# Moving the second half of a value projection, and spreading output-weight splits and turned rows, in a fused hybrid decoder layer

## The chip, the cores and the metric

The kernel runs on one core of a Trainium2 chip. The metric is the device time of one execution in microseconds (us). Five engines work side by side, each through its own queue in order: TensorE (PE; matmuls and transposes, its weight loads are listed as PEld), VectorE (DVE), ScalarE (ACT), GpSimd (POOL) and SyncE (SP), which issues the DMAs. The trace is that of one profiled execution.

## What is computed

The layer takes x (1024 tokens of 1024 values, float32). The reference, cut to what matters here:

```python
h = rmsnorm(x, mix_pre_norm)
proj = h @ w_in
q_a, k_a, v_a, q_h, f_h, i_h, g_h = split(proj)
attn = rmsnorm(dilated_mixture_attention(q_a, k_a, v_a, slopes), attn_out_norm)   # 8 heads of 64
rec = hgrn2_recurrence(q_h, f_h, i_h, g_h, lower_bounds, hgrn_out_norm)           # 4 heads of 128
mixed = concatenate([attn, rec]) @ w_out
x = x + rmsnorm(mixed, mix_post_norm)
h = rmsnorm(x, mlp_pre_norm)
x = x + rmsnorm(square(relu(h @ w_ff1)) @ w_ff2, mlp_post_norm)
```

The three dilated windows of the attention are one causal softmax with a table of biases per head, so that a head's block of 128 queries has scores against all earlier keys. The product is float32: each operand is split in a high part (float32r) and the rest, and three matmuls make one product (`three_pass`, L86: high x high, high x low, low x high).

## The kernel before, in words

The whole layer is one function, `hymba_layer`, and the order of all work is written out by hand: each engine gets its instructions in the order in which the program names them. Four stages follow each other: the recurrent heads, the attention loop (from about 314 to 564 us), the output projection with the norms, and the feed-forward part.

**The attention loop** (L970 to L996) has 64 steps: head `hd` = step // 8, block `b` = step % 8 of 128 queries. In step s the program names, in this order: the exponentials of step s + 1 on ACT (`raise_`); the scores of step s + 2, two matmuls per 512 keys on PE, then bias and maximum on DVE (`look`, `score`, L660); the transposes of step s's probabilities on PE, with the high part taken out of the bank by ACT (L708) and the low part by DVE (L709) (`turn`); after odd blocks, a step later, the product with the values (`weigh`, L713), and another step later its transposes back (`finish`, L728), which DVE sums (`anat`, L737) and POOL scales (L738). Then come the step's *hook*, if it has one, and `fill`.

**Filler.** `fill(ns)` (L170) takes pieces of work from a queue of generators. It adds ns to a debt and calls the first generator until the yielded costs have used the debt up; what a piece costs too much is carried to the next step, and what is left when the queue is empty is forgotten. `drain` (L183) runs the queue empty. Before, a step's budget is 3400 - 360 b up to step 43, 1000 in steps 44 to 47, and 1300 from step 48.

The filler of a pair of heads is the next pair's projection, `attn_proj` (L583): query, value and key, each for two halves of 512 tokens (`proj_t`, L329: eight pieces of three matmuls, cost 650 each). DVE scales each finished half by the row norms (`qf`, `vf`, `kf`). A value half is also transposed on PE (`v_turn`, L605, bank `pvt`), and ACT (L611) and DVE (L612) write its high and low parts to `v`. In both value halves that turn stands some pieces after the scaling (L618, L637). A key half goes through `keys_off` (L570): DVE's scaling, two copies on ACT (L576), two subtractions on POOL (L577), four DMA copies. The second key half of a pair waits in `put_off` until a block 7, 0 or 1 (L993). The last pair (number 3, heads 6 and 7, steps 48 to 63) is projected from step 30 on; its scores begin with `look(48)` in step 46, and values of the second half of the tokens are first needed in step 54.

When the last pair's first key half is done, `early_rows` (L755) puts into the space of the first half of the normed input the finished recurrent rows of 512 tokens (`erows`), a gain row, and room for turned rows (`emt`).

**The output projection's first half** is the filler of the last pair: `early_out` (L837), for four blocks of 128 tokens and two halves of the columns, four pieces each (32 in all, cost 650), multiplies a turned recurrent row with output-weight tiles 0 to 3. It needs the rows multiplied by their gain (`row_rec`, L781, POOL), turned (`row_turn`, L811: four transposes on PE into a bank of tag `t`, one of two that the probabilities' transposes use as well; split by ACT and DVE into `emt`), and the weight tiles split.

**Weights** come through one stream (L95 to L164): `w_load` issues the DMA of a tile into one of two buffers `raw`, `w_split` splits it (ACT L83, DVE L84) into the tile that the stream names for it and issues the next load, and `w_get(i, ahead)` (L123) splits up to tile i + ahead. Where the stream names no tile, the parts go to `wh` and `wl`, two buffers each; the output weights have `WO_TAG` (L154) for that.

**The hooks** (L953) are a table of what each step names after its attention work. Those around the change:

Of the kernel before, what the change touches and what calls it, by code (L numbers as in the profile page):

```python
# [12 lines left out]
ALU = mybir.AluOpType  # L13
# [5 lines left out]
T = 1024  # L19
# [6 lines left out]
AH = 8  # L26
# [9 lines left out]
def hymba_layer(ctx, tc, x, w_in, w_out, w_ff1, w_ff2, g_pre, lb_logits, g_mix, g_post,  # L36
                g_mlp, g_mlp_post, bias_tab, level_masks, ident_in, fold_in, out):
    nc = tc.nc
    V, S, G, TE = nc.vector, nc.scalar, nc.gpsimd, nc.tensor
# [18 lines left out]
    def half(name, dtype=F32):  # L58
        return sp.tile([P, 512], dtype, tag="half", name=name, bufs=2)
# [63 lines left out]
    def w_get(i, ahead=1):  # L123
        while done[1] < min(i + 1 + ahead, len(stream)):
            w_split()
        return parts[i]
# [17 lines left out]
    for h in range(HH):  # L144
        dest, box = pair_dest(f"wig{h}")
# [5 lines left out]
    for i in range(4 * HH, 4 * HH + 3 * (AH // 2)):  # L151
        stream.append((w_in[i], None))
    WO0 = len(stream)
    WO_TAG = (None, ("S", "S"), None, ("S", "BT"), ("S", "S"), ("S", "T"), ("T", "T"), ("T", "T"))  # L154

    def wo_dest(k, tags):
        return lambda: (slab(tags[0], f"woh{k}", F32R), slab(tags[1], f"wol{k}", F32R))
# [9 lines left out]
    queue = []  # L167
    debt = [0.0]

    def fill(ns):  # L170
        debt[0] += ns
        while debt[0] > 0 and queue:
            try:
                cost = next(queue[0])
            except StopIteration:
                queue.pop(0)
                continue
            if cost is None:
                break
            debt[0] -= cost  # L180
        debt[0] = min(debt[0], 0.0)

    def drain():  # L183
        while queue:
            n = len(queue)
            fill(1e9)
            assert len(queue) < n or not queue
# [141 lines left out]
    def proj_t(w, name, hf, out_box):  # L329
        wh, wl = kc(w[0]), kc(w[1])  # L330
        pm = bank("mm", f"pm_{name}{hf}")
        for k in range(NK):
            three_pass(pm, (wh[:, k], wl[:, k]), part(hT, k, hf), k == 0, k == NK - 1)
            out_box[0] = pm
            if k < NK - 1:
                yield 650.0
# [228 lines left out]
    first_done = [False] * (AH // 2)  # L565
    A0 = 4 * HH

    put_off = []

    def keys_off(pr, stacks, pm, hf):  # L570

# [11 lines left out]
    def attn_proj(pr):  # L583
        stacks = [{}, {}]
        box = [None]
        w = w_get(A0 + 3 * pr)
        for i in range(2):
            stacks[i]["q"] = slab("S", f"q{pr}_{i}", F32R)
        for hf in range(2):
            sl = slice(hf * 512, hf * 512 + 512)  # L590
            yield from proj_t(w, f"aq{pr}", hf, box)
            full = half(f"qf{pr}{hf}")
            V.scalar_tensor_tensor(full, box[0], 0.125, rrow[:, sl], op0=ALU.mult, op1=ALU.mult)
            lo = half(f"ql{pr}{hf}", F32R)
            for i, (a, b) in enumerate(halves):
                S.activation(stacks[i]["q"][a:b, sl], full[a:b], AF.Copy)
                G.tensor_tensor(out=lo[a:b], in0=full[a:b], in1=f32(stacks[i]["q"][a:b, sl]), op=ALU.subtract)
            nc.sync.dma_start(out=f32(stacks[0]["q"][64:128, sl]), in_=f32(lo[0:64]))
            nc.sync.dma_start(out=f32(stacks[1]["q"][0:64, sl]), in_=f32(lo[64:128]))
            yield 650.0  # L600
        w = w_get(A0 + 3 * pr + 1)
        vs = slab("V8", f"v{pr}", F32R, (P, NT, 2, 2, 64))
        late = None

        def v_turn(full, hf):  # L605
            pt = bank("mm", f"pvt{pr}{hf}")
            for j in range(4):
                TE.transpose(pt[:, j * P:(j + 1) * P], full[:, j * P:(j + 1) * P], ident)
            ptv = pt.rearrange("p (j h d) -> p j h d", j=4, h=2)
            dst = vs[:, hf * 4:hf * 4 + 4]  # L610
            S.activation(dst[:, :, :, 0, :], ptv, AF.Copy)  # L611
            V.tensor_tensor(out=dst[:, :, :, 1, :], in0=ptv, in1=f32(dst[:, :, :, 0, :]), op=ALU.subtract)  # L612
        for hf in range(2):
            sl = slice(hf * 512, hf * 512 + 512)
            n = 0
            for cost in proj_t(w, f"av{pr}", hf, box):
                n += 1
                if n == 4 and late is not None:  # L618
                    v_turn(*late)
                    cost += 450.0  # L620
                yield cost
            full = half(f"vf{pr}{hf}")
            V.tensor_tensor(out=full, in0=box[0], in1=rrow[:, sl], op=ALU.mult)
            late = (full, hf)
            yield 650.0
        while pr > 0 and not first_done[pr - 1]:
            yield None
        w = w_get(A0 + 3 * pr + 2)
        for i in range(2):
            stacks[i]["kh"] = slab("S", f"kh{pr}_{i}", F32R)  # L630
            stacks[i]["kl"] = slab("S", f"kl{pr}_{i}", F32R)
        for hf in range(2):
            sl = slice(hf * 512, hf * 512 + 512)
            n = 0
            for cost in proj_t(w, f"ak{pr}", hf, box):
                n += 1
                if n == 3 and hf == 0:  # L637
                    v_turn(*late)
                    cost += 450.0
                yield cost  # L640
            if hf == 0 and pr == AH // 2 - 1:
                early_rows()
            if hf == 0 or pr == 0:
                keys_off(pr, stacks, box[0], hf)
            else:
                put_off.append((pr, stacks, box[0], hf))
            pairs[pr] = (stacks, vs)
            yield 650.0
# [6 lines left out]
    def load_bias(hd):  # L655
        if hd < AH and hd not in bts:
            bts[hd] = slab("BT", f"bt{hd}") if hd < AH - 1 else early["table"][:, 0]
            nc.sync.dma_start(out=bts[hd], in_=bias_tab[hd])
# [89 lines left out]
    def load_gain(name, tag, src):  # L748
        gains[name] = slab(tag, name)
        nc.sync.dma_start(out=gains[name], in_=src.partition_broadcast(P))  # L750
# [16 lines left out]
    def early_sums():  # L767
        early["sum"] = [wide.tile([P, 2, D], F32, tag="A", name=f"esum{q}") for q in range(NE // 2)]
# [12 lines left out]
    def row_rec(t):  # L781
        gain = gains["early"] if t < NE else gains["gmix"][:, :AW]
        G.tensor_tensor(out=rec_row(t), in0=rec_row(t), in1=gain, op=ALU.mult)
# [27 lines left out]
    def row_turn(t, which, late=False):  # L811

        if t < NE and which == 0:
            dst = early["mt"][t // 2][:, t % 2]
        else:
            if (t, 1) not in mts and (t, 0) not in mts or t < NE:
                mts[t] = slab("V8", f"mt{t}", F32R, (P, 2, 2, 4, P))
            dst = mts[t][:, which]
        mts[t, which] = dst
        src = rec_row(t) if which == 0 else rows[t][:, AW:]  # L820
        pt = bank("pv" if late else "t", f"pmt{t}_{which}")
        for j in range(4):
            TE.transpose(pt[:, j * P:(j + 1) * P], src[:, j * P:(j + 1) * P], ident)
        split_into(dst[:, 0], dst[:, 1], pt.rearrange("p (j c) -> p j c", j=4))
# [119 lines left out]
    for h in range(HH):  # L944
# [5 lines left out]
        if not last:  # L950
            drain()

    hooks = {  # L953
        45: lambda: [row_rec(0), row_rec(1)],
        46: lambda: [w_get(WO0, 0), row_rec(2), row_rec(3)],
        47: lambda: [row_turn(0, 0), w_get(WO0 + 1, 0), load_bias(AH - 1)],
        48: lambda: [drain(), load_gain("gmix", "R", g_mix), early_sums(), w_get(WO0 + 2, 0), row_turn(1, 0),
                     queue.extend(early_out(t) for t in range(NE))],
        49: lambda: [w_get(WO0 + 3, 0), row_turn(2, 0)],
        50: lambda: row_turn(3, 0),  # L960
        55: lambda: [row_load(t) for t in range(3)],
        59: lambda: [row_norm(0), row_gain(0)],
        60: lambda: [row_norm(1), row_gain(1)],
# [6 lines left out]
    for s in range(n_steps):  # L970
        if s % 16 == 6:
            first_done[s // 16] = True
        hd, b = steps[s]
        ready, to_weigh = to_weigh, []
        raise_(s + 1)
        fresh = (s + 2) % 16 == 0
        if not fresh:
            look(s + 2)
        turn(hd, b, exped.pop(s))
        if b % 2:  # L980
            to_weigh.append((hd, b // 2))
        to_fold, last_fold = [(i, g, weigh(i, g)) for i, g in ready], to_fold
        if fresh and s + 2 < n_steps:
            while pairs[(s + 2) // 16] is None:
                fill(1.0)
            if (s + 2) // 16 + 1 < AH // 2:
                drain()
                queue.append(attn_proj((s + 2) // 16 + 1))
            look(s + 2)
        for i, g, a in last_fold:  # L990
            finish(i, g, *a)
        hooks.get(s, lambda: None)()
        if b in (7, 0, 1):  # L993
            while put_off:
                keys_off(*put_off.pop())
        fill(3400.0 - 360.0 * b if s < n_steps - 20 else 1000.0 if s < n_steps - 16 else 1300.0)  # L996
    for i, g, a in to_fold:
        finish(i, g, *a)
    to_fold = [(i, g, weigh(i, g)) for i, g in to_weigh]
# [804 lines left out]
```

## Time and profile before

| | |
|---|---|
| median of 3 runs | 1278.68 us (1278.18 to 1279.29) |
| profiled execution | 1281.3 us |
| its span, from the first to the last instruction | 1279.2 us |
| mean granted clock of TensorE | 0.994 |
| DMA | 153.98 MB, mean 120 GB/s |
| weight-tile split on ACT, 128 x 1024 (L83, `woh`) | 1.06 us each |
| weight-tile split on DVE, 128 x 1024 (L84, `wol`) | 1.22 us each |

How to read the views. A row of a group or of the timeline has the line of the kernel, the engine, the operation, what it writes and reads by the program's names without their numbers, the size, and (in brackets) how long the engine was idle before it and what ended that. In a timeline row the first two numbers are the start and the length, in us from the start of the span; instructions of one kind that follow each other are one row with a count. A row of the windows view has its two ends and its length, then the busy time of PE (and, where all engines are shown, of PEld, DVE, ACT and POOL) with a count, the granted clock, the share of the DMA engines and GB/s. The page's clock row has one digit for each fortieth of the span, 9 for 90% or more. A DMA row ends with the kilobytes of one issue and the median time to its landing. Matmuls overlap in the records, so that a matmul's length is more than the distance to the next one's start.

### The profile page before, as it was taken

How to read it: one execution, taken by the hardware profiler on the slowest of the kernel's cores; microseconds unless marked ns; L12 is line 12 of the kernel's file. 1: busy time of each engine (PE TensorE's matmuls, PEld its weight loads, DVE VectorE, ACT ScalarE, POOL GpSimd, SP SyncE). 2: the span in 40 equal slices, each digit the busy share in tenths (PEclk: the TensorE clock that was granted, in tenths of full speed). 3: DMA queues.
4: the chain of work that ended last, by engine and by line, in shares of the span. 5: the costliest groups of instructions: out<-in, count | busy, mean ns of one | idle time of the engine just before them, and what ended most of it. 6: DMA issues, size and time to landing. Idle time of an engine off the chain costs nothing. (4 is left out here: it accounts for less than half of the span.)

```text
span 1279.2 us, 17265 instructions
## 1 busy us (share of the span) xinstructions
PE 1243.7 (97%) x6512; PEld 1059.0 (83%) x6512; DVE 884.4 (69%) x1530; ACT 533.2 (42%) x969; POOL 291.2 (23%) x304
## 2 busy tenths in 40 slices
PE   9999999999999998999999999999999999999997
PEld 8898989888888887787888888888878888888886
DVE  5686868675666666666668767666675776698956
ACT  7523232213555555564565322222235533344412
POOL 0000000012122223134351387566541000000002
PEclk9999999999999999898999999999999999999999
DMA  5201111123232223326242544344369453534413
GB/s 207 67 17 50 34 51 33 34 82 84 66 83 67 79 71 94 116 90 204 83 166 91 174 172 170 137 170 152 140 242 354 148 200 130 164 99 132 155 68 140
DMA packets 58578, 153.98 MB, mean 120 GB/s; under 512 B 4992, under 2 KB 12928, under 8 KB 58240
## 3 DMA queue, kind: packets, MB, share of 16 engines
q1 hardware_dynamic: 58496, 152.89, 35.8%
q8 instruction: 51, 0.84, 0.3%
q14 instruction: 31, 0.25, 0.1%
HBM read 106.73 MB, written 39.85 MB: 115 GB/s over the span
## 5 line engine op out<-in xcount | busy, mean ns | idle before, releaser
L87 PE MATMUL f<-bh,ah 128*128 128x512 f32 x392 | 152.5, 389 | 0.0
L88 PE MATMUL f<-bl,ah 128*128 128x512 f32 x392 | 152.5, 389 | 0.0
L89 PE MATMUL f<-bh,al 128*128 128x512 f32 x392 | 152.5, 389 | 0.0
L84 DVE TENSOR_TENSOR al<-ar,ah 128x1024 fp32r<-128x1024 f32 x49 | 60.6, 1236 | 48.1 <-ACT ah L83 17.7
L88 PEld LDWEIGHTS f<-bl,ah 128*128 128x128 f32 x392 | 73.6, 188 | 15.4
L87 PEld LDWEIGHTS f<-bh,ah 128*128 128x128 f32 x392 | 73.6, 188 | 15.2
L89 PEld LDWEIGHTS f<-bh,al 128*128 128x128 f32 x392 | 73.6, 188 | 15.1
L83 ACT ACTIVATE ah<-ar 128x1024 fp32r<-128x1024 f32 x49 | 52.1, 1063 | 49.3 <-DMA ar<-actd 20.5
L1719 POOL TENSOR_SCALAR fp<-fss 128x1 f32<-128x1 f32 x8 | 3.5, 434 | 267.4 <-ACT fd L1716 267.4
L681 DVE CUSTOM_DVE_ANT_0 p<-ps,bt 128x512 f32<-128x512 f32 (+2 forms) x84 | 44.3, 552 | 24.2 <-PE ps L679 24.0
L709 DVE TENSOR_TENSOR ptl<-pt,pth 128x512 fp32r<-128x512 f32 (+2 forms) x96 | 50.2, 551 | 15.6 <-ACT pth L708 15.6
L708 ACT ACTIVATE pth<-pt 128x512 fp32r<-128x512 f32 (+2 forms) x96 | 43.3, 486 | 41.7 <-PE pt L705 40.0
L692 ACT ACTIVATE p<-p,nm 128x128 f32<-128x128 f32 (+3 forms) x64 | 49.5, 773 | 9.5 <-DVE nm L687 6.2
L1232 POOL TENSOR_TENSOR e<-x,e 128x512 f32<-128x512 f32 x14 | 20.6, 1475 | 136.3 <-DVE x L1183 136.3
L738 POOL TENSOR_TENSOR anat<-anat,rd 128x128 f32<-128x128 f32 x32 | 14.6, 455 | 150.1 <-DVE anat L737 146.5
L83 ACT ACTIVATE bh<-br 128x1024 fp32r<-128x1024 f32 x28 | 29.8, 1063 | 43.5 <-PE f L89 38.2
L79 POOL TENSOR_SCALAR ms<-hss 128x8 f32<-128x8 f32 x4 | 0.8, 198 | 206.3 <-DVE hss L549 206.3
L705 PE MATMUL pt<-ident,p 128*128 128x128 f32 x288 | 42.9, 276 | 4.7 <-DVE ptl L709 4.7
L84 DVE TENSOR_TENSOR wl<-raw,wh 128x1024 fp32r<-128x1024 f32 x23 | 31.4, 1365 | 18.3 <-ACT wh L83 18.0
L705 PEld LDWEIGHTS pt<-ident,p 128*128 128x128 f32 x288 | 33.5, 141 | 9.3 <-DVE ptl L709 6.8
L722 PE MATMUL pov<-pth,v 128*128 128x256 f32 (+1 forms) x160 | 40.6, 288 | 0.0
L1586 DVE TENSOR_TENSOR acc<-f,acc 128x512 f32<-128x512 f32 x52 | 33.8, 685 | 8.3 <-PE f L89 8.3
(1615 smaller groups left out, 3892.1 us busy)
## 6 DMA issues: line engine op xcount, KB each, us to landing
ar<-actd SPq DMA_DIRECT2D x49, 512.0 KB, 3.6
raw<-in_w_in_dram SPq DMA_DIRECT2D x28, 512.0 KB, 3.5
w1r<-in_w_ff_dram SPq DMA_DIRECT2D x14, 1024.0 KB, 6.3
br<-in_w_ff_dram SPq DMA_DIRECT2D x14, 1024.0 KB, 7.8
actd<-e SPq DMA_DIRECT2D x17, 768.0 KB, 4.1
actd<-e SPq DMA_DIRECT2D x11, 1024.0 KB, 4.0
xr<-in_x_dram SPq DMA_DIRECT2D x8, 512.0 KB, 9.4
raw<-in_w_out_dram SPq DMA_DIRECT2D x8, 512.0 KB, 3.7
```

What stands on the lines that cost most here:

```text
L83: S.activation(hi, src, AF.Copy)
L84: eng.tensor_tensor(out=lo, in0=src, in1=f32(hi), op=ALU.subtract)
L87: TE.matmul(dst, lhs[0], rhs[0], start=start, stop=False)
L88: TE.matmul(dst, lhs[0], rhs[1], start=False, stop=False)
L89: TE.matmul(dst, lhs[1], rhs[0], start=False, stop=stop)
L681: V.tensor_tensor_reduce(out=pe[:, k0:k0 + n], in0=pS[:, :n], in1=bts[hd][:, o:o + n], scale=1.0, scalar=-3.0e38, op0=ALU.add, op1=ALU.max ...
L692: S.activation(pe[:, :nk], pe[:, :nk], AF.Exp, bias=nm[:, b:b + 1], accum_out=dn[:, b:b + 1])
L705: TE.transpose(pt[:, j * P:(j + 1) * P], pe[:, jj * P:(jj + 1) * P], ident)
L708: S.activation(hi, src, AF.Copy)
L709: V.tensor_tensor(out=lo, in0=src, in1=f32(hi), op=ALU.subtract)
L722: TE.matmul(po[:, c0:256], vst, pt[j // 4][q][:, j % 4, c0:], start=j == 0 and q == 0, stop=j == nj - 1 and q == 1)
L1586: V.tensor_tensor(out=acc_at(p, i), in0=pm, in1=acc_at(p, i), op=ALU.add)
```

## The change

The last pair's value projection of the second half of the tokens is taken out of `attn_proj` into a generator of its own, `v_rest`, which step 45 puts into the queue after draining it; `v_turn` follows its scaling directly. The hooks that were in steps 45 to 50 are spread over steps 43 to 53, with one weight tile or one turned row in most of them. The tiles of `wh` and `wl` go to output-weight tiles 2 and 3 instead of 0 and 2, since the value weights now stay in theirs up to step 48, and the last key weights are fetched without one ahead. The second key half is also taken off in step 46. The budgets change: 2660 - 280 b in steps 30 to 43, 1000 in steps 44 and 45, and 1500 from step 46.

```diff
-    WO_TAG = (None, ("S", "S"), None, ("S", "BT"), ("S", "S"), ("S", "T"), ("T", "T"), ("T", "T"))
+    WO_TAG = (("S", "S"), ("S", "BT"), None, None, ("S", "S"), ("S", "T"), ("T", "T"), ("T", "T"))
...
-    put_off = []
+    put_off, deferred = [], []
...
-        for hf in range(2):
+        split = pr == AH // 2 - 1
+
+        def v_rest(wv):
+            sl = slice(512, T)
+            yield from proj_t(wv, f"av{pr}", 1, box)
+            full = half(f"vf{pr}1")
+            V.tensor_tensor(out=full, in0=box[0], in1=rrow[:, sl], op=ALU.mult)
+            yield 650.0
+            v_turn(full, 1)
+            yield 450.0
+        if split:
+            deferred.append(v_rest(w))
+        for hf in range(1 if split else 2):
...
-        w = w_get(A0 + 3 * pr + 2)
+        w = w_get(A0 + 3 * pr + 2, 0 if split else 1)
...
-        45: lambda: [row_rec(0), row_rec(1)],
-        46: lambda: [w_get(WO0, 0), row_rec(2), row_rec(3)],
-        47: lambda: [row_turn(0, 0), w_get(WO0 + 1, 0), load_bias(AH - 1)],
-        48: lambda: [drain(), load_gain("gmix", "R", g_mix), early_sums(), w_get(WO0 + 2, 0), row_turn(1, 0),
+        43: lambda: [row_rec(0), row_rec(1)],
+        44: lambda: [row_rec(2), row_rec(3)],
+        45: lambda: [drain(), queue.append(deferred.pop())],
+        46: lambda: load_bias(AH - 1),
+        47: lambda: w_get(WO0, 0),
+        48: lambda: row_turn(0, 0),
+        49: lambda: w_get(WO0 + 1, 0),
+        50: lambda: [drain(), load_gain("gmix", "R", g_mix), early_sums(), w_get(WO0 + 2, 0), row_turn(1, 0),
                      queue.extend(early_out(t) for t in range(NE))],
-        49: lambda: [w_get(WO0 + 3, 0), row_turn(2, 0)],
-        50: lambda: row_turn(3, 0),
+        51: lambda: w_get(WO0 + 3, 0),
+        52: lambda: row_turn(2, 0),
+        53: lambda: row_turn(3, 0),
...
-        if b in (7, 0, 1):
+        if b in (7, 0, 1) or s == 46:
             while put_off:
                 keys_off(*put_off.pop())
-        fill(3400.0 - 360.0 * b if s < n_steps - 20 else 1000.0 if s < n_steps - 16 else 1300.0)
+        if s < n_steps - 20:
+            fill(3400.0 - 360.0 * b if s < n_steps - 34 else 2660.0 - 280.0 * b)
+        else:
+            fill(1000.0 if s < n_steps - 18 else 1500.0)
```

## The prediction

> **What bounds the kernel now.** I read the page first: busy shares, then the clock row.
>
> ```profile
> span 1279.2 us, 17265 instructions
> ...
> PE 1243.7 (97%) x6512; PEld 1059.0 (83%) x6512; DVE 884.4 (69%) x1530; ACT 533.2 (42%) x969; POOL 291.2 (23%) x304
> ...
> PEclk9999999999999999898999999999999999999999
> ```
>
> TensorE sets the time: it is idle for only 1279.2 - 1243.7 = 35.5 us. A change that neither adds nor removes matmuls, as this one, can win only idle time of PE and time at a lowered clock. One of the two dips of the clock row (slice 17, from 512 us) lies in the attention loop. So I cut the windows view at the steps of that loop (steps 46, 47 and 49; each begins with its score matmuls), and took the idle times of PE from its timeline.
>
> ```profile
> 499.26:502.65 3.39, 2.41 (x22) 2.42 (x22) 2.70 (x10) 2.58 (x6) 1.67 (x3) 1.00 0.00 0
> 502.65:505.56 2.91, 1.93 (x19) 1.72 (x18) 2.25 (x10) 1.85 (x5) 2.91 (x3) 1.00 0.00 0
> ...
> 509.79:518.14 8.35, 4.13 (x17) 2.50 (x16) 5.51 (x13) 6.32 (x15) 3.78 (x3) 0.85 1.02 303
> ```
>
> ```profile
> 500.24 0.98 PE L705 MATMUL pt<-ident,p 128*128 128x128 f32 x7 [0.98 <-DVE ptl L709]
> 505.18 0.63 PE L823 MATMUL pmt<-ident,erows 128*128 128x128 f32 x4 [0.98 <-POOL erows L783]
> 511.72 0.44 PE L705 MATMUL pt<-ident,p 128*128 128x128 f32 x2 [1.32 <-DVE ptl L709]
> 514.52 0.63 PE L823 MATMUL pmt<-ident,erows 128*128 128x128 f32 x4 [2.14 <-issue]
> 514.91 0.48 PE L87 MATMUL pwe<-wh,emt 128*128 128x512 f32 x1
> ...
> 517.12 0.79 PE L88 MATMUL pwe<-wol,emt 128*128 128x512 f32 x1 [0.75 <-DVE wol L84]
> ```
>
> Steps 46 and 47 have no filler matmuls, and PE waits 0.98 us in each. In step 49 it waits 1.32, 2.14 and 0.75 us. Together 6.17 us. What it waits for in step 49 stands in the timelines of DVE and ACT:
>
> ```profile
> 508.56 0.68 DVE L574 TENSOR_TENSOR kf<-pm_ak,rrow 128x512 f32<-128x512 f32 x1
> ...
> 512.60 1.22 DVE L84 TENSOR_TENSOR wl<-raw,wh 128x1024 fp32r<-128x1024 f32 x1 [0.86 <-ACT wh L83]
> 513.74 0.68 DVE L84 TENSOR_TENSOR emt<-pmt,emt 128x512 fp32r<-128x512 f32 x1
> ...
> 515.86 1.21 DVE L84 TENSOR_TENSOR wol<-raw,woh 128x1024 fp32r<-128x1024 f32 x1
> ```
>
> ```profile
> 509.27 1.28 ACT L576 ACTIVATE kh<-kf 64x512 fp32r<-64x512 f32 x2 [1.89 <-DVE kf L574]
> ```
>
> The 1.32 us come from the second half of the keys: ACT stands 1.89 us for `kf` and then works 1.28 us before it gets to the next weights. The 2.14 us ("issue" in the row) end when DVE, done with a weight tile at 513.8, has emptied the bank of the row turned before (`emt`, to 514.42). The 0.75 us end with `wol` at 517.07: an output-weight tile whose split stands in the step that first uses it. Then comes the clock. In PE's windows, cut where the clock changed:
>
> ```profile
> 501.96:505.37 3.41, 2.43 (x22) 1.00 0.00 0
> 505.37:508.79 3.42, 3.42 (x29) 1.00 0.01 2
> 508.79:512.20 3.41, 2.09 (x12) 1.00 0.73 227
> 512.20:515.61 3.41, 1.27 (x9) 1.00 1.07 273
> 515.61:519.03 3.42, 2.67 (x8) 0.50 0.99 332
> 519.03:522.44 3.41, 3.41 (x16) 0.50 0.79 251
> ...
> 594.12:597.53 3.41, 1.44 (x10) 1.00 0.98 310
> ```
>
> After a window with 1.27 us of PE work the granted clock is 0.50 for 6.83 us. Of these PE is idle 0.75, so 6.08 us of work run at half speed and cost 3.04 us. The other dip follows 1.44 us of work; 2.09 and 2.43 us of work caused none. **The prize is 6.17 + 3.04 = 9.2 us**, between 499 and 523 us.
>
> **The change part by part.** PE's work is the same. A filler piece (three matmuls of 512 columns) is the distance of these starts, 0.69 us:
>
> ```profile
> 479.20 0.39 PE L87 MATMUL pm_av<-hTh,wh 128*128 128x512 f32 x1
> ...
> 479.89 0.39 PE L87 MATMUL pm_ak<-hTh,wh 128*128 128x512 f32 x1
> ```
>
> *Steps 30 to 43, fewer pieces.* Counting the new budgets (costs 650 a piece, debts carried) gives 2, 1, 4, 4, 3, 3, 2, 2, 2, 1, 3, 4, 3, 3, 1 pieces in steps 30 to 44 (40 with step 45's two) instead of 2, 2, 5, 5, 4, 3, 3, 3, 1, 1, 6, 4, 4, 3, 2 (48). Where DVE has most to do (steps 37 to 39) at most one is lost. The thin place is the change of weights from query to value, where before PE waits once already:
>
> ```profile
> 461.20 0.50 PE L678 MATMUL ps<-kh,q 128*128 128x512 f32 x1 [1.17 <-DVE mx L681]
> ```
>
> The second query half now ends a step later and has about 0.4 us less PE work behind it before a score needs DVE: +0.4 us, bounds 0 and +1.2 (the wait once more).
>
> *Steps 45 to 47.* Two key pieces and two value pieces, then two, then three: 2.76, 1.38 and 2.07 us of cover where there was none, and the row gains on POOL end four steps before the first row is turned. The two waits of 0.98 us go. The keys' second half moves to step 46, ahead of the crowd, so the 1.32 us go too. What moves onto other queues (the last number is the time to landing):
>
> ```profile
> raw<-in_w_out_dram SPq DMA_DIRECT2D x3, 512.0 KB, 5.1
> erows<-mixd SPq DMA_DIRECT2D x2, 512.0 KB, 8.1
> ...
> kl<-kl SPq DMA_DIRECT2D x4, 128.0 KB, 4.7
> ```
>
> The row gains stand on POOL two steps earlier, behind rows that take 8.1 us to land: POOL waits there, and of what is queued behind it PE needs nothing before step 50. The keys' copies have four steps for their 4.7 us. The load of the fourth output tile leaves when the second is split (step 49) and lands 5.1 us later, about when its split comes up; a microsecond late costs PE as much. It now stands ahead of the gain row's load on SP's queue, which nobody needs before step 59.
>
> *Step 48.* By the budgets the last value piece and the turn of it (`v_turn`) come straight one after the other. Before, three pieces lay between them:
>
> ```profile
> 480.09 0.69 DVE L623 TENSOR_TENSOR vf<-pm_av,rrow 128x512 f32<-128x512 f32 x1 [2.47 <-PE pm_av L89]
> ...
> 483.20 0.69 DVE L612 TENSOR_TENSOR v<-pvt,v 128x512 fp32r<-128x512 f32 x1 [1.02 <-ACT v L611]
> ```
>
> ```profile
> 482.57 0.60 ACT L611 ACTIVATE v<-pvt 128x512 fp32r<-128x512 f32 x1 [1.64 <-PE pvt L608]
> ```
>
> Now PE waits for `vf`, 0.69 us, and DVE first empties the turned row of this step (`emt`, 0.68 us, some of it beside the piece). **+1.3 us**, bounds 0.7 (`vf` alone) and 2.0 (both and an output split of 0.6 us still running).
>
> *Steps 49 to 51.* The queue is empty in step 49, and the splits of the second, third and fourth output-weight tiles stand in steps 49, 50 and 51. The budgets let step 50 issue pieces 0, 1 and 2 of the first early row block, and step 51 piece 3: tiles three and four are used in the very step that splits them, and before only the fourth was. Steps 57 to 59 do the same attention work with two pieces each (PE, PEld, then DVE busy):
>
> ```profile
> 543.24:545.53 2.29, 2.29 (x14) 1.90 (x12) 1.58 (x6) 1.32 (x5) 0.00 (x0) 1.00 0.00 0
> 545.53:548.36 2.83, 2.83 (x18) 2.49 (x17) 1.66 (x7) 1.81 (x6) 0.40 (x1) 1.00 0.00 0
> 548.36:551.08 2.72, 2.72 (x17) 2.39 (x16) 2.02 (x8) 1.61 (x5) 0.00 (x0) 1.00 0.00 0
> ```
>
> DVE's chain to the end of the fourth split: 1.58 + 1.66 + 2.02 = 5.3, and 0.3 of `anat` cut off at 551.08; three splits of 1.22 = 3.7; a turned row 0.68; the rest of the value turn 0.69. That is 10.7 us, begun 0.60 us late (ACT's `v`), with about 0.5 us of waiting for scores: 11.8 us. PE's work ahead of the matmul that needs that split: (2.29 + 2.83 + 2.72) - 6 x 0.69 = 3.7; a turned row 0.39 (514.52 to 514.91); three pieces 2.07; one matmul 0.23: 6.4 us. So PE stands **5.4 us** in these steps, in holes of 0.7 to 1.8 us, the largest at tiles three and four. Bounds: 2.7 (half, if DVE enters step 49 ahead of PE) and 7 (ACT's splits late as well).
>
> *The clock.* Twelve microseconds with 6.4 us of work, the last four of them with little but turns: some window of 3.41 us holds under 1.5 us of work wherever the windows begin, and at 1.27 and 1.44 us the clock fell. So it falls again, near the end of step 51: +3.2 us (6.83 us at half, little idle within; before it was 3.04). Bounds 0 and 6.4 (twice).
> The Trainium skill ("TensorE: Matmul & The Clock Gate", section "HAM oscillation — how this bites in real kernels") gives as its rule no idle gaps over some 3.4 us. By that rule none of these holes would lower the clock, and the sum would be 3.2 us less. This trace speaks against it: 2.14 us was the longest hole ahead of 515.61.
>
> *Steps 52 to 63.* Two to three pieces a step instead of two, the same 32 in all, ending in the same step; PE is busy throughout there. The turns of rows three and four have full steps around them. Nothing.
>
> **The sum**: -6.17 - 3.04 + 0.4 + 1.3 + 5.4 + 3.2 = **+1.1 us**. In the profiled execution (1281.3 us with a span of 1279.2) that is a span of 1280.3; the median of the runs, 1278.68, becomes **1279.8 us**. Waits are not removed but moved: DVE takes the place of ACT and POOL as what PE waits for.
>
> **The rivals.**
> *It does what it says.* The value pieces let DVE run ahead, the holes of steps 49 to 51 halve, the clock holds: -9.2 + 0.4 + 1.3 + 2.7 = -4.8, 1273.9 us. For it: steps 45 to 47 do get cover. Against: DVE's own work in 49 to 51 exceeds PE's, and no piece is left for step 49. 12%.
> *The holes come, the clock holds* (the rule named above): -2.1, 1276.6 us. For it: the holes are several and short, and 2.09 us of work in a window left the clock alone. Against: the window at 594 us. 19%.
> *Slower: the clock falls twice*, first at the end of step 48, where a turned row, the wait for `vf` and the value turn leave one piece and one score in some 4 us, and again after step 51: +3.2 more, 1283.0 us. It decides when both windows are under about 1.5 us of work. For it: the two places are ten microseconds apart, more than the 6.83 us of one dip. Against: the first hole is barely long enough. 21%.
>
> **The numbers.** My forecast has 48%, with its own range 1277.8 to 1281.9 (the bounds of the hole terms, not all at once). A measurement of this kernel can tell about 0.2%, 2.6 us: 1276.1 to 1281.2. Faster: the first rival and a third of the second, 0.18. Slower: the third rival and a quarter of the forecast's 48%, 0.33. The same: the rest, 0.49. The range that should hold 8 in 10 reaches from 1275.4 (second rival with smaller holes) to 1283.5 (third rival and a little more), and leaves the first rival out.
>
> **What would show it.** Right: no idle time of PE on `erows` or `ptl` in steps 46 and 47; an idle time of about 1 us ahead of `pvt` in step 48; waits for `wl` in steps 50 and 51 of 1 us or more; a stretch at clock 0.50 beginning within steps 50 to 52. Wrong: a clock of 1.00 all through the loop, or PE busy over 90% in steps 49 to 51; then the time is nearer 1274. Waits for `mx` over 2 us in steps 35 to 38 would make it slower than all of this.

## The result and the profile after

The changed kernel took 1281.73 us (median of 18 executions, 1279.33 to 1283.40), the kernel before beside it 1278.93 us (18 executions). The ratio is 1.0016, with a 95% interval of 1.0010 to 1.0022: **slower by 0.16%, some 2 us** (the two medians lie 2.8 us apart). A second measurement of both kernels gave 1.0021 (1.0011 to 1.0031). The forecast was 1279.8 us in a range of 1275.4 to 1283.5.

The profiled execution of the changed kernel has a span of 1280.0 us and took 1281.8 us. These are all idle times of PE over 0.15 us from 436 to 560 us in its timeline; L717, L693 and L835 of this kernel are L705, L681 and L823 of the one before:

```profile
462.66 0.50 PE L690 MATMUL ps<-kh,q 128*128 128x512 f32 x1 [1.59 <-DVE mx L693]
...
507.23 0.66 PE L608 MATMUL pvt<-ident,vf 128*128 128x128 f32 x4 [1.33 <-DVE vf L619]
509.90 0.33 PE L690 MATMUL ps<-kh,q 128*128 128x128 f32 x1 [0.65 <-DVE mx L693]
514.67 0.50 PE L88 MATMUL pwe<-wl,emt 128*128 128x512 f32 x1 [1.49 <-DVE wl L84]
518.18 0.50 PE L87 MATMUL pwe<-wh,emt 128*128 128x512 f32 x1 [1.41 <-ACT wh L83]
519.48 0.79 PE L88 MATMUL pwe<-wl,emt 128*128 128x512 f32 x1 [0.80 <-DVE wl L84]
525.08 0.66 PE L835 MATMUL pmt<-ident,erows 128*128 128x128 f32 x4 [0.41 <-DVE ptl L721]
529.90 0.66 PE L835 MATMUL pmt<-ident,erows 128*128 128x128 f32 x4 [0.98 <-DVE ptl L721]
...
558.58 0.63 PE L835 MATMUL pmt<-ident,row 128*128 128x128 f32 x4 [1.07 <-DVE ptl L721]
```

The five waits of before in steps 46 to 49 (6.17 us) are gone. In their place stand seven in steps 48 to 53: 1.33 + 0.65 + 1.49 + 1.41 + 0.80 + 0.41 + 0.98 = 7.07 us. The wait in step 37 (462.66) has grown from 1.17 to 1.59 us. The DVE timeline shows how the two waits for `wl` come about: in step 50 DVE gets to the low part of tile 2 only after the scores and the probabilities of its steps, and ends it at 514.62; in step 51 that of tile 3 at 519.43. PE goes on at 514.67 and 519.48.

```profile
511.81 0.68 DVE L693 CUSTOM_DVE_ANT_0 p<-ps,bt 128x512 f32<-128x512 f32 x1
...
512.88 0.55 DVE L721 TENSOR_TENSOR ptl<-pt,pth 128x384 fp32r<-128x384 f32 x1
513.34 0.15 DVE L723 RECIPROCAL rd<-dn 128x1 f32<-128x1 f32 x1
513.41 1.21 DVE L84 TENSOR_TENSOR wl<-raw,wh 128x1024 fp32r<-128x1024 f32 x1
...
518.21 1.22 DVE L84 TENSOR_TENSOR wl<-raw,wh 128x1024 fp32r<-128x1024 f32 x1
```

The 1.41 us are a wait for ACT. It stands 2.66 us for the transposes of step 51, which PE reaches only after its own wait for tile 2, and takes the high part of tile 3 right behind them:

```profile
516.58 0.60 ACT L720 ACTIVATE pth<-pt 128x512 fp32r<-128x512 f32 x1 [2.66 <-PE pt L717]
517.08 1.05 ACT L83 ACTIVATE wh<-raw 128x1024 fp32r<-128x1024 f32 x1
```

The load of that tile was issued at 512.65, after the split of tile 1 had made a buffer `raw` free, and took 4.3 us to land, to 516.94: 0.14 us ahead of the split. Where PE and ACT get there sooner it holds the split up, as in e_late.

PE's windows of 3.41 us, cut where this execution's clock changed (window, length, PE busy with its count, granted clock, DMA share, GB/s):

```profile
512.57:515.98 3.41, 1.92 (x10) 1.00 0.92 283
515.98:519.39 3.41, 1.29 (x9) 1.00 0.99 330
519.39:522.80 3.41, 3.32 (x8) 0.50 0.50 155
522.80:526.21 3.41, 3.00 (x23) 1.00 0.00 0
594.49:597.90 3.41, 1.48 (x11) 1.00 0.93 328
```

The clock falls again, after a window with 1.29 us of work, but for one window and not for two. Between two instructions that both kernels have (the transposes of step 30 after the wait at 435.6 us, and the first attention row's turn in step 61), the windows view gives, for the kernel before and then the changed one (length, PE, PEld, DVE, ACT and POOL busy, clock):

```profile
435.62:557.82 122.20, 113.59 (x678) 98.66 (x679) 78.65 (x244) 71.65 (x164) 29.68 (x40) 0.97 0.30 85
```

```profile
435.62:558.58 122.96, 113.11 (x678) 97.57 (x679) 78.25 (x244) 71.73 (x164) 31.53 (x40) 0.99 0.29 85
```

The 0.76 us between the two lengths are the 0.8 us between the two spans, so the difference lies in this stretch. Idle time of PE rose from 8.61 to 9.85 us (+1.24), and its busy time fell by 0.48. Half clock cost 3.04 us before and 1.66 us now (half of the 3.32 us of work in the slow window), so the clock favours the changed kernel here by 1.38 us. At an equal clock the stretch is 0.76 + 1.38 = 2.1 us longer: 1.24 us of idle time, and 0.9 us by which the same 678 instructions kept PE busy longer. Where those 0.9 us come from stays open; the second profile of the changed kernel (after_again) has them too. Over many executions the clock favours neither kernel: the mean granted clock is 0.9953 in the 18 of the changed one and 0.9954 in 33 of the one before. So the result is these 2.1 us, as much as the measured 0.16%, and somewhat over half of it is idle time.

### The profile page after: what moved, and what is told of

Same layout as the page of the kernel before. It is cut to its first block, busy times and chain, and to the rows that moved or that the text cites. A ratio compares the mean times of both kernels' runs of the same rounds, so it can differ in the third digit from the quotient of the medians.

```text
span 1280.0 us, 17268 instructions
## 1 busy us (share of the span) xinstructions
PE 1243.1 (97%) x6512; PEld 1058.0 (83%) x6512; DVE 883.1 (69%) x1530; ACT 533.1 (42%) x969; POOL 293.2 (23%) x304
## 5 line engine op out<-in xcount | busy, mean ns | idle before, releaser
L693 DVE CUSTOM_DVE_ANT_0 p<-ps,bt 128x512 f32<-128x512 f32 (+2 forms) x84 | 44.3, 552 | 28.1 <-PE ps L691 27.9
L717 PE MATMUL pt<-ident,p 128*128 128x128 f32 x288 | 42.5, 274 | 2.4 <-DVE ptl L721 2.3
L717 PEld LDWEIGHTS pt<-ident,p 128*128 128x128 f32 x288 | 33.4, 140 | 6.8 <-DVE ptl L721 4.1
```

The costliest lines, as they stand in the source:

```text
L693: V.tensor_tensor_reduce(out=pe[:, k0:k0 + n], in0=pS[:, :n], in1=bts[hd][:, o:o + n], scale=1.0, scalar=-3.0e38, op0=ALU.add, op1=ALU.max ...
L717: TE.transpose(pt[:, j * P:(j + 1) * P], pe[:, jj * P:(jj + 1) * P], ident)
```

## The experiments

The theory at the start: each wait has a cause of its own (a tile used in the step that splits it; a turn right behind its scaling; a row turned in a step that uses both banks), and the time follows their sum. The first rival: DVE's work in steps 46 to 53 is the bound, and a wait that is taken away comes back elsewhere. The second: the windows at half clock decide. "Waits" is the sum of PE's idle times over 0.15 us in steps 46 to 53 of each profile, and so of one execution.

| kernel | median us | ratio to the kernel before, run beside it | waits us |
|---|---|---|---|
| before | 1278.9 to 1280.1 | 1 | 6.17 |
| changed | 1281.73 | 1.0016 (1.0010 to 1.0022) | 7.07 |
| after_again | 1282.47 | 1.0021 (1.0011 to 1.0031) | 7.08 |
| e_turn | 1281.29 | 1.0010 (1.0001 to 1.0019) | 4.94 |
| e_rows | 1281.46 | 1.0005 (0.9997 to 1.0014) | 6.18 |
| e_late | 1282.02 | 1.0020 (1.0009 to 1.0031) | 7.02 |
| e_late_rows | 1275.87 | 0.9976 (0.9965 to 0.9986) | 3.46 |
| e_warm | 1280.71 | 1.0008 (1.0000 to 1.0017) | 3.87 |
| e_pool | 1284.30 | 1.0044 (1.0032 to 1.0057) | 9.71 |
| b_keys | 1279.21 | 0.9991 (0.9982 to 1.0000) | 5.54 |
| b_pool | 1279.42 | 1.0003 (0.9994 to 1.0012) | 6.20 |
| c_spread | 1276.77 | 0.9977 (0.9968 to 0.9987) | 2.36 |
| c_pool | 1272.94 | 0.9955 (0.9943 to 0.9967) | 1.57 |
| c_pool2 | 1273.14 | 0.9952 (0.9938 to 0.9965) | 0.42 |

**e_turn: the value turn in the next step.**

```diff
             yield 650.0
+            yield None
             v_turn(full, 1)
```

> The changed kernel, but the last value piece and its turn stand in different steps: v_turn is named in step 49 instead of right behind its scaling in step 48. Theory of the holes (each wait of PE is a cost of its own): the 1.33 us ahead of pvt in the profile of the changed kernel goes, and step 49 gets 0.35 us of PE work; about 1.3 us faster than the changed kernel, 1280.4 us. Theory of a bound DVE (DVE's work in steps 47 to 51 sets the end whatever PE does): the wait turns up again at the score or the weight tile after it, 1281.7 us, and the waits of steps 50 and 51 add up to 1 us more than before (they were 0.65 + 1.49 + 1.41 + 0.80).

The wait ahead of `pvt` fell from 1.33 to 0.43 us, the score's 0.65 and the first row turn's 0.41 went, and those for tiles changed little: 2.1 us less waiting. The time did not follow: 1.0010, not to be told from the changed kernel's 1.0016. What may have taken it back stands in the windows of its profile:

```profile
512.29:515.70 3.41, 1.59 (x7) 1.00 1.00 297
515.70:519.11 3.41, 2.21 (x10) 0.50 0.88 274
519.11:522.52 3.41, 2.90 (x7) 0.50 0.51 138
522.52:525.93 3.41, 3.41 (x14) 0.50 0.16 64
```

The clock fell one window earlier, and as the next two windows had waits of their own, it stayed at half for 10.24 us. Over its 11 executions the mean clock was 0.9938 (changed kernel 0.9953); 0.0015 of 1280 us is 1.9 us, about what the waits had given. The two sizes agree; that the one paid for the other was not tested further.

**e_rows: the third and fourth rows turned in steps 56 and 57.**

```diff
-        52: lambda: row_turn(2, 0),
-        53: lambda: row_turn(3, 0),
+        56: lambda: row_turn(2, 0),
+        57: lambda: row_turn(3, 0),
```

> The changed kernel, but the third and fourth turned rows stand in steps 56 and 57 instead of 52 and 53. Theory of the holes: the waits of 0.41 and 0.98 us ahead of pmt come because steps 52 and 53 (blocks 4 and 5) turn more than four blocks and so use both banks of the tag t, and go in steps with one bank: 1.4 us faster than the changed kernel, 1280.3 us. Rival: they are only the remainder of DVE's delay from step 51 (DVE is late there in any case), and PE then waits as long at the scores of steps 53 to 55: 1281.7 us.

The two waits of 0.41 and 0.98 us went and nothing took their place in steps 52 to 60; the waits for tile 3 grew by 0.50 us together, and the sum fell by 0.9. The ratio is 1.0005; its interval overlaps that of the changed kernel, so the 1.4 us are seen in the trace and not settled by the time.

**e_late: tiles 2 and 3 used a step after their split.**

```diff
-            fill(1000.0 if s < n_steps - 18 else 1500.0)
+            fill({50: 1300.0, 51: 600.0}.get(s, 1000.0 if s < 46 else 1500.0 if s < 52 else 1580.0))
```

> The changed kernel, but the first early row block gets two pieces in step 50 and one in step 51, so that output-weight tiles 2 and 3 are used a step after the one that splits them (the other 29 pieces in steps 52 to 63). Theory of the holes: the waits for wl and wh (1.49, 1.41 and 0.80 us) go or fall under 0.5 us each, 2.5 to 3.7 us; steps 50 and 51 are then short of PE work, and half of it comes back as waits for scores (mx): net 1.5 us faster than the changed kernel, 1280.2 us. Theory of a bound DVE: all of it comes back, 1281.7 us. If the lowered clock is what counts, it is seen in the number of 3.41 us windows at half speed: one fewer is worth 1.7 us.

The rival had the number: 1.0020, and waits of 7.02 us. The three waits for tiles went, and one of 3.58 us came:

```profile
516.02 0.50 PE L690 MATMUL ps<-kh,q 128*128 128x512 f32 x1 [0.48 <-DVE mx L693]
...
522.11 0.66 PE L835 MATMUL pmt<-ident,erows 128*128 128x128 f32 x4 [3.58 <-DVE ptl L721]
```

The third row's turn needs a bank of tag `t`. Step 52's own transposes have taken both, and DVE empties them (`ptl`, 521.38) only after tile 3's split and the scores of step 54. So PE met the end of DVE's queue. But that end was not late by DVE's own work: DVE stood 1.35 us for tile 3's high part, and ACT, which makes it, 2.90 us for the tile's load, issued at 512.80 and landed 5.0 us later.

```profile
517.81 1.06 ACT L83 ACTIVATE wh<-raw 128x1024 fp32r<-128x1024 f32 x1 [2.90 <-DMA raw<-in_w_out_dram]
518.90 1.23 DVE L84 TENSOR_TENSOR wl<-raw,wh 128x1024 fp32r<-128x1024 f32 x1 [1.35 <-ACT wh L83]
521.38 0.88 DVE L721 TENSOR_TENSOR ptl<-pt,pth 128x512 fp32r<-128x512 f32 x2
```

**e_late_rows: both edits.**

> The two edits of e_late and e_rows together. In e_late the waits for tiles went and came back as one of 3.58 us ahead of the third turned row (step 52) for a bank that DVE empties (ptl). If DVE's delay is the bound, moving that row moves the wait again, to a score or a piece in step 52, and the waits of steps 48 to 53 still add up to 7 us; as e_late, 1282 us. If it was the pair of banks, 3 to 4 us of waits go, 1278.5 us.

The waits fell to 3.46 us and the ratio to 0.9976: some 5 us faster than the changed kernel, where one edit alone gave 0 and about 1 us. **The two causes hid each other**: whoever removes one meets the other behind it. Of the 5 us, 3.6 are waits. The mean clock rose too, to 0.9974 (2.7 us by the reckoning of e_turn), so the shares are not clean. DVE's sum does not explain it, as DVE has the same work in all four kernels. A third cause is left in: the load of tile 3 still holds ACT for 2.73 us, and PE waits 0.23 and 0.77 us for that tile. No run moved the load alone.

**e_warm: needless matmuls in the waits.**

```diff
             wh, wl = parts[WO0 + n]
+            if (t, hf) == (0, 0) and n in (2, 3):
+                if n == 2:
+                    early["junk"] = bank("pv", "junk")
+                jh, jl = parts[WO0]
+                for _ in range(n):
+                    three_pass(early["junk"], (mt[:, 0, 0], mt[:, 1, 0]), (jh[:, sl], jl[:, sl]), True, True)
```

> The changed kernel with five pieces of needless matmuls (0.69 us each) in the waits for tiles 2 and 3: two ahead of piece 2 in step 50, three ahead of piece 3 in step 51, into a bank that nobody reads; the output is the same. If the waits cost only their own length, nothing changes (the needless work fits into 1.49 and 2.2 us of waiting; up to 0.3 us slower). If the clock counts, fewer windows run at half speed around 519 us: mean clock 0.0005 to 0.0015 higher and the time 0.6 to 2 us lower than the changed kernel.

The matmuls fit into the waits (what is left for tiles is 0.49 us), and the mean clock of 11 executions rose from 0.9953 to 0.9973, more than expected. The ratio went from 1.0016 to 1.0008; the intervals overlap, so a gain of about 1 us is likely and not shown, and it is less than the 2.6 us that 0.0020 of clock would be. Work that computes nothing raised the clock and made the kernel no slower: the waits cost clock beside their own length.

**e_pool: POOL takes the low parts of tiles 0 to 3.**

```diff
-    def w_get(i, ahead=1):
+    def w_get(i, ahead=1, eng=V):
...
-            w_split()
+            w_split(eng)
...
-        47: lambda: w_get(WO0, 0),
+        47: lambda: w_get(WO0, 0, G),
```

and so in the hooks of the other three tiles.

> The changed kernel with one edit: the low parts of output-weight tiles 0 to 3 are subtracted by POOL instead of DVE (about 2.5 us each, where DVE takes 1.22); order and budgets are those of the change. Theory that the waits of steps 49 to 53 are DVE's sum: DVE loses 4.9 us there, the waits for scores (0.65) and for the banks of turned rows (0.41 and 0.98) go or halve, and the time falls by 2 us or more, to 1279.5 us. Theory that what counts is the use of a tile in the step of its split: the waits for wl in steps 50 and 51 (1.49 and 0.80) grow by up to 1.3 us each, as POOL is slower, and outweigh it: 1282 to 1283 us.

Slower by 0.44% than the kernel before. The waits for tiles 1, 2 and 3 became 1.14, 1.36 and 1.41 + 2.44 us; those for a score and for the banks stayed to 0.01 us. DVE had 4.9 us less to do and nothing was won: in the order of the change, the time from a tile's split to its use counts, not DVE's sum. The rival of a bound DVE falls for this order; for another one see c_pool.

**b_keys: two small parts of the change alone, on the kernel before.**

```diff
-        45: lambda: [row_rec(0), row_rec(1)],
-        46: lambda: [w_get(WO0, 0), row_rec(2), row_rec(3)],
+        43: lambda: [row_rec(0), row_rec(1)],
+        44: lambda: [row_rec(2), row_rec(3)],
+        46: lambda: w_get(WO0, 0),
...
-        if b in (7, 0, 1):
+        if b in (7, 0, 1) or s == 46:
```

> The kernel before with two small parts of the change alone: the row gains stand in steps 43 and 44, and the second key half is taken off in step 46; the value projection, the weight tiles, the turned rows and the budgets are those of before. Theory of the holes: the waits of 0.98 us on erows (step 47) and of 1.32 us in step 49 go, 2.3 us, and the 2.14 us behind them stays for the most part; 1276.6 us, faster than both kernels. Theory of a bound DVE: it has the same work in steps 46 to 49, so PE waits as long a little later: 1278.9 us.

Some 1 us instead of the expected 2.3: 0.9991, waits 5.54. The 1.32 us went and the 2.14 us shrank to 0.63, but ahead of the first turned row PE now waits 2.89 us instead of 0.98, since the keys' two copies on ACT stand ahead of step 47's probabilities, and DVE waits for those:

```profile
503.28 0.68 DVE L574 TENSOR_TENSOR kf<-pm_ak,rrow 128x512 f32<-128x512 f32 x1
...
506.31 1.29 DVE L709 TENSOR_TENSOR ptl<-pt,pth 128x512 fp32r<-128x512 f32 x2 [1.82 <-ACT pth L708]
```

**c_spread: the work of the change, spread otherwise.** Value pieces thinner and up to step 49, tiles 0 and 1 split one and two steps earlier and in steps with fillers, rows turned in steps of one bank, tiles 2 and 3 used a step after their split.

```diff
-        46: lambda: load_bias(AH - 1),
-        47: lambda: w_get(WO0, 0),
+        46: lambda: [load_bias(AH - 1), w_get(WO0, 0)],
+        47: lambda: w_get(WO0 + 1, 0),
         48: lambda: row_turn(0, 0),
-        49: lambda: w_get(WO0 + 1, 0),
+        49: lambda: row_turn(1, 0),
...
-        52: lambda: row_turn(2, 0),
-        53: lambda: row_turn(3, 0),
+        56: lambda: row_turn(2, 0),
+        57: lambda: row_turn(3, 0),
...
-            fill(1000.0 if s < n_steps - 18 else 1500.0)
+            fill({44: 1000.0, 45: 650.0, 46: 650.0, 51: 600.0}.get(s, 1300.0 if s < 52 else 1580.0))
```

(The hook of step 50 loses its row turn.)

> The changed kernel with its work spread otherwise: value pieces one, one, two, two and two in steps 45 to 49, the value turn in step 50, weight tiles 0 and 1 split in steps 46 and 47, rows turned in steps 48, 49, 56 and 57, early pieces two in step 50, one in step 51 and 29 in steps 52 to 63. Theory that DVE's work in the steps is the bound: DVE has the same work from step 46 on but PE has pieces in every step, so of the 7.1 us of waits in steps 48 to 53 some 3 remain; 4 us faster than the changed kernel and 1.5 faster than the one before, 1278.5 us on this chip (before 1280.0). Rival (what counts is the use of a tile in the step of its split, and the turns): nearly all waits go, 1275 us. Rival of the clock: whatever the waits, the time follows the number of windows at half speed.

Faster than both kernels, and between the two forecasts: 0.9977. The clock did not do it: its mean is 0.9944, below the changed kernel's 0.9953, so the rival of the clock falls. One wait is left, 2.36 us ahead of step 48's transposes: ACT and DVE have tile 0's split and the second keys in the same step. Since tile 1 is split in step 47 here, the load of tile 3 leaves at 506.69 and has landed more than 7 us ahead of its split (517.78). How much of the gain is due to that, the runs do not separate.

**c_pool and c_pool2: low parts on POOL, in that order.** c_pool is c_spread with the edit of e_pool for all four tiles, c_pool2 for tiles 0 and 1 only.

> As c_spread, but the low parts of output-weight tiles 0 to 3 are subtracted by POOL instead of DVE (some 2.5 us each by the row gains' 1.25 us for half the size). Theory that DVE is the bound of steps 46 to 51: DVE loses 4 x 1.22 = 4.9 us there, and the waits that c_spread still has go by up to that: 2 to 3 us faster than c_spread. Rival (single late uses, not DVE's sum): the tiles are ready 1.3 us later each, so the waits for them grow, and the time is c_spread's or 1 us more.

> As c_pool, but only the low parts of tiles 0 and 1 (steps 46 and 47) go to POOL; tiles 2 and 3 are split by DVE again. c_pool still waits 1.15 us for POOL's low part of tile 2, and 0.42 us ahead of step 48's transposes (2.36 in c_spread, where DVE splits all four). If the delay of DVE at step 48 comes from tiles 0 and 1 alone, 0.42 stays, the 1.15 goes and nothing takes its place: 1272 us, 1 us faster than c_pool. If DVE is still the bound in steps 50 and 51, 1.2 us or more comes back there: 1273 us or above.

c_pool: 0.9955 (0.9943 to 0.9967), 5.8 us faster than the kernel before; c_pool2 the same within the intervals. POOL takes twice as long as DVE for a tile and it costs little, as the tiles are now split a step or more ahead of their use; step 48's wait shrinks to 0.42 us. Here the theory of a bound DVE had the better forecast (2 to 3 us faster than c_spread; 0.9955 against 0.9977 is 2.8): once no tile is used in the step of its split, what DVE has to do does count. The waits give 0.8 us of the 2.8. The mean clock is 0.9975 in six executions against c_spread's 0.9944, which would be more than the rest, so the shares are open. c_pool2 removes the 1.15 us that c_pool waits for tile 2 and is not measurably faster. In c_pool's profile (span 1271.0 us) PE waits, of steps 46 to 53, in steps 48 and 51 only, and the clock is 1.00 from start to tail:

```profile
500.99 0.33 PE L717 MATMUL pt<-ident,p 128*128 128x128 f32 x1 [0.42 <-DVE ptl L721]
513.65 0.50 PE L88 MATMUL pwe<-wl,emt 128*128 128x512 f32 x1 [1.15 <-POOL wl L84]
```

```profile
435.45:549.40 113.95, 109.61 (x676) 96.03 (x676) 73.64 (x240) 71.48 (x164) 38.40 (x44) 1.00 0.32 91
```

The stretch that took 122.96 us takes 113.95.

**b_pool: the same medicine without the value projection.** b_keys with POOL splits in steps 47 to 49, rows turned in steps 48, 49, 51 and 57, and budgets 650, 650 and 1300 in steps 48 to 50, 1420 after.

> The kernel before, with what c_pool does apart from the value projection: row gains in steps 43 and 44, second key half in step 46, tiles split by POOL in steps 47 to 49, rows turned in steps 48, 49, 51 and 57, early pieces one, one and two in steps 48, 49 and 50. The value projection stays where it was, and steps 45 to 47 have no filler. If moving the value half is what makes c_pool possible (cover in steps 45 to 49): PE waits 4 to 5 us in steps 46 to 50, 1277 to 1278 us (before 1279.5). If the order of tiles and turned rows alone did it: within 1 us of c_pool, 1273 us.

1.0003: no gain, waits of 6.20 us (0.98, 2.50, 0.84, 1.88). So this order of tiles and rows, on POOL, gains nothing without the value half as filler in steps 45 to 47. That speaks for the idea of the change, and for its placement as what lost it; b_pool differs from c_pool in the early pieces and the budgets as well.

**after_again: the changed kernel once more.**

> The changed kernel once more, on the chip and beside the runs of the same call: whether its place against the kernel before holds (ratio 1.0016 so far), and how often its time falls into each of its two groups (six of 18 executions under 1280.5 us, twelve over 1281). By the theory that the two groups differ in one window at half speed, they lie 1.7 us apart at equal work, and the mean clock of the upper group is 0.001 to 0.002 lower.

1.0021, and its profile has the same waits to 0.02 us. The groups are there but not clean: nine executions run from 1280.68 to 1284.00 us with clocks of 0.994 to 0.999, and one at 0.999 took 1281.11 us. In the 18 executions of the first measurement a lower clock goes with a longer time (0.996 or more: 1279.33 to 1281.63 us; 0.995 or less: 1281.16 to 1283.40). That one window separates two groups is not shown.

## Why the prediction was right, and where it was wrong

*The waits that go*: all five went, as forecast.

*Steps 30 to 43*: +0.4 forecast; 1.59 against 1.17 us, +0.42.

*The value turn in step 48*: +1.3 forecast, 1.33 measured.

*Steps 49 to 51*: 5.4 us forecast at scores and tiles 2 and 3; 0.65 + 1.49 + 1.41 + 0.80 = 4.35 us measured, at these places. The places were right, the size 1.05 too large. The reason given, that DVE's chain is longer than PE's work, was the weaker half. The chain was reckoned without gaps, but DVE itself stands 0.69 us for scores behind PE's wait for tile 2 (515.91 in its timeline), and 1.41 of the 4.35 us are for ACT. e_pool took 4.9 us from DVE, and no wait for a score or a bank shrank; e_late_rows kept DVE's work and won. The other half, tiles used in the step of their split, was the one that counted in this order.

*The load of the fourth output tile* was forecast to land about when its split comes up. It did, 0.14 us ahead. The warning that went with it came true in e_late, where it held ACT for 2.90 us.

*Steps 52 to 63*: "The turns of rows three and four have full steps around them. Nothing." This step failed. They wait 0.41 and 0.98 us, since blocks 4 and 5 turn five and six blocks of probabilities and take both banks. Before, those rows were turned in steps 49 and 50, which use one. And in e_late it was this, behind the load of tile 3, that held the whole gain back.

*The clock*: -3.04 and +3.2 were forecast. It fell where forecast, near the end of step 51 (519.39), but in the profiled execution this cost 1.7 us (one window at half). The first was real in the execution that was profiled and not typical: that one took 1281.3 us, and of 33 executions of the kernel before only ten had a mean clock of 0.994 or less, the others 0.996 or more. Of the 18 of the changed kernel eleven are at 0.995 or less. The prediction read a term of 3 us off one execution of the kernel before, one with a low clock; that is why the two profiles differ by 0.8 us where the medians differ by 2.8. In the sum the two clock terms all but cancel (+0.16), and so do the mean clocks: there the net was right, by luck rather than by its parts.

*The sum*: idle time +0.4 + 1.3 + 5.4 - 6.17 = +0.9 forecast, +1.24 measured over the whole stretch. The two misses (1.05 too much, 1.39 forgotten) nearly cancelled, which is luck. "PE's work is the same" put a further term at nothing: at an equal clock PE's busy time grew by 0.9 us, and no run shows why. With it the change costs the 2.1 us of the measured ratio, where the forecast had 1.1.

*The rivals*: "It does what it says" was refused by the changed kernel and borne out by its relatives: the 4.8 us it named are there (c_pool 5.8), for another arrangement and with POOL's help. "The holes come, the clock holds" was refused too: the clock fell, though no hole of steps 48 to 51 is over 1.49 us. What e_warm imitates of it, the clock kept up in spite of the holes, took 1280.7 us and not 1276.6. The clock falling twice was seen in no profile of the changed kernel, and in e_turn as one fall three windows long.

## What to carry to other kernels

Before moving filler work under a wait, list for the new place what each step uses that the same step produces (a split tile, a scaled half, an emptied bank), and put a step between the two; the slower engine may then do it at little cost. List also when each load can leave: here a tile's load waited for the split of the tile two before it. When an edit removes a wait and the time stays, look in the trace for what PE met next and remove both before judging: here two edits worth 0 and about 1 us alone were worth some 5 together, clock included. Do not take a clock loss from one execution for the kernel's; count it over many.

## What the runs showed of the hardware

**When the clock falls.** The slow stretches are 3.41, 6.83 or 10.24 us long, and two falls in one profile lie a whole number of 3.41 us apart (24 in the kernel before, 515.61 and 597.53; 23 in the changed one, 519.39 and 597.90). So each profile can be cut into windows of 3.41 us. In the 14 profiles the clock fell 23 times ahead of the last 20 us, each time at the end of a window in which PE was busy for 0.50 us (e_pool, from 517.89) to 1.75 us (e_turn, from 461.09); the windows at full clock with 1.82 us or more kept it. A fall ended after a slow window with 2.86 to 3.41 us of work and went on after one with 2.21 to 2.90. The longest single hole need not be long. In c_pool2 one of 1.59 us at 462.65 sufficed, since it fell into one window; the changed kernel's equal hole, in windows that lie otherwise, did not (its clock is 1.00 there):

```profile
460.92:464.33 3.41, 1.70 (x8) 1.00 0.58 143
464.33:467.74 3.41, 3.41 (x13) 0.50 0.52 165
```

The limit is not sharp: e_late has three windows of 1.60, 1.66 and 1.73 us without a fall. The place of the windows differs from execution to execution (in the two profiles of the changed kernel by 0.48 us), so the same hole can cost 1.7 us or nothing.

**Transposes count as work there.** The window 433.70 to 437.11 of the kernel before holds 2.43 us, all but some 0.8 us of it transposes, and the clock stayed. Without them it would count as a window of 0.8 us, and every window with 1.54 us or less lost the clock:

```profile
433.70:437.11 3.41, 2.43 (x23) 1.00 0.36 108
```

**A tile's low part** took 2.4 us on POOL (c_pool) where DVE takes 1.22:

```profile
503.50 2.40 POOL L84 TENSOR_TENSOR wol<-raw,woh 128x1024 fp32r<-128x1024 f32 x1
```
